# A two-layer diffusion trunk: decay tables and modulation begun in the first stage, HGRN2 scores by halves of a chunk

## The chip, the core and the metric

The kernel runs on one core of a Trainium2 chip. The metric is the device time of one launch in microseconds (us). The core's engines work side by side, each through its own queue in order: PE (TensorE, matrix products), DVE (VectorE), ACT (ScalarE), POOL (GpSimd) and SP (SyncE, which here only issues DMAs). A weight load of PE is shown apart as PEld.

## The reference, cut to what matters

640 tokens (512 latent ones, then a context of 128) pass through two layers of width 1024. In each layer a vector made from a condition (the modulation: six parts of 1024 values, for latents and for context) shifts, scales and gates the stream. Three kinds of heads read one input projection: Fourier mixing, retention, and HGRN2, whose state has a forget gate of its own in every channel. Then come an output projection and a gated feed-forward net.

```python
def _modulation(cvec, w_mod_l, b_mod_l):
    m = jax.nn.silu(cvec) @ w_mod_l + b_mod_l
    return jnp.split(m[..., None, :], N_MOD, axis=-1)

# HGRN2, one chunk: b = running sum of log f
rel = bc[:, :, :, None, :] - bc[:, :, None, :, :]
dec = jnp.exp(jnp.where(tri[:, :, None], rel, -jnp.inf))
A = jnp.sum(qc[:, :, :, None, :] * kc[:, :, None, :, :] * dec, axis=-1)
o = inter + jnp.einsum('bhij,bhjv->bhiv', A, vc)
S = (jnp.exp(b_last[:, :, 0, :])[..., None] * S
     + jnp.einsum('bhjd,bhjv->bhdv', kc * jnp.exp(b_last - bc), vc))
```

Retention has one fixed decay per head and direction instead: `lg = -exp(log_decay)`, from which tables of `exp(distance * lg)` are made. Both run over the sequence forward and backward.

## The kernel before, in words

**Precision.** Most products are made as three matmuls of a high and a low part (`mm3`, L219 to L221). A weight tile is loaded into `wraw` (one of two buffers), ACT casts it to `whi` (L206) and DVE subtracts to get `wlo` (L207). Products in plain f32, those of the HGRN2 and retention heads among them, show two PE records for each call.

**The stages.** The initial stage (`trunk`, from 0 to about 66 us) normalizes the five token tiles, makes shift and scale of layer 0 with matmuls (`weights`, L248), transposes and modulates (`norm`, L371 to L383), and projects the first values (`part`). It goes over four quarters `q` of the width, with five parts in each. Then `mixers` runs the heads of layer 0 (to about 345 us), `feed` the output projection and the feed-forward net; then both again for layer 1, whose mixers lie between about 920 and 1175 us.

**The order.** PE's instructions stay in the order in which the program writes them. The other engines' are put in order by a scheduler, which prefers what the program writes first. The program's order comes from a planner (`Order`, `run_units`): it has a clock `now`, which units of work on PE move on by an estimate (`pe`), and threads, each of which goes on when its due time has come (`due`). The modulation of layer 0's other parts is such a thread: `modulation(0, (2, 3, 4), pace0)` starts at the beginning of `mixers` and takes a step every 2.8 us of the planner's clock. It goes through two halves of the condition; each half has two steps that load and prepare the condition vectors (`csb`, with a sigmoid on ACT into `junk`) and 24 pieces. A piece is a 256 KB load through SP into one of three `wm` buffers and two multiplications with a running sum on DVE (L312, L314).

**HGRN2 scores.** `hgrn` (from L766) is a thread for each of three pairs of heads over the latents (four chunks of 128 tokens, `nu` = 4) and one for the context (three pairs, `nu` = 3). A chunk's 128x128 scores are put together by levels: the diagonal (`pd`, L809), then for `lev` 0 to 6 the scores between neighbouring blocks of 2^lev tokens. At each level PE multiplies the composite keys `C` with the queries `Qx`, 128 columns at a time (L824, one call for each chunk and head: a matmul of 64 rows, 128 weights columns and 128 columns); POOL multiplies the keys and the decay products (L832, L835); ACT makes the next composite (L799); DVE multiplies the queries in place (L839); and of the 128x128 products the blocks that the level is about are put into `AT`: by DVE with a mask for lev 0 to 4 (`copy_predicated`, L843), by ACT block by block for lev 5 and 6 (L847). The next level's matmuls need the `Qx` of L839.

**Decay tables.** `decays` (L656 to L686) is called by the first retention unit in the program's order, in each layer. It loads a small table `ctab` through SP, computes `ea`, `ec`, `gam` and `zt` with exponentials on ACT and small multiplications on DVE (L665 to L675), then the large tables `G` and `DT`.

Of the kernel before, what the change touches and what calls it, by code (L numbers as in the profile page):

```python
# [151 lines left out]
class Kernel:  # L152
    def __init__(self, ctx, tc, a, outs):
        self.tc, self.nc, self.a, self.outs = tc, tc.nc, a, outs
        nc = tc.nc
        PS = bass.MemoryType.PSUM
        self.const = ctx.enter_context(tc.tile_pool(name="const", bufs=1))
        self.wp = ctx.enter_context(tc.tile_pool(name="wp", bufs=1))
        self.actp = ctx.enter_context(tc.tile_pool(name="actp", bufs=1))
        self.psp = ctx.enter_context(tc.tile_pool(name="psp", bufs=8, space=PS))  # L160
        dram = ctx.enter_context(tc.tile_pool(name="dram", bufs=1, space=bass.MemoryType.DRAM))
        self.mem = Slots()
        self.get, self.free, self.can = self.mem.get, self.mem.free, self.mem.can
        self.mem.add(self.wp, "wr", 4096, 2)
        self.mem.add(self.wp, "wh", 4096, 4)
        self.mem.add(self.wp, "wl", 4096, 4)
        self.mem.add(self.actp, "ax", 4 * T, 16)
        self.mem.add(self.actp, "m4", 4096, 8)
        self.xd = dram.tile([T, D], F32, name="xd")
        self.gd = dram.tile([L, 2, 2, D], F32, name="gd")  # L170
        c = self.const

        def load(name, shape, eng=nc.gpsimd):
            t = c.tile(list(shape), F32, name=name)
            eng.dma_start(t, a[name])
            return t

        self.cvec = load("cvec", [128, NK, 2], nc.sync)
        self.ident = load("ident", [128, 128], nc.scalar)
        self.bmf = load("bmf", [128, L, 6, NK], nc.scalar)  # L180
        self.bonesr = c.tile([128, 128], F32R, name="bonesr")
        nc.gpsimd.dma_start(self.bonesr, a["bones"])
        self.bones = self.bonesr.bitcast(F32)
        self.lda = load("lda", [128, L, 2, 6])
        self.ldc = load("ldc", [128, L, 3, 2])
        self.hlb = load("hlb", [128, 2, 2, 3])
        self.mhalf = c.tile([128, 1], F32, name="mhalf")
# [277 lines left out]
    def mixers(self, l, hT, mp):  # L465
# [7 lines left out]
        self.raws, self.mix = [None] * 6, [None] * NK  # L473
        mskf = self.m4("mskf", (128, 7, 128))
        nc.sync.dma_start(mskf, a["masks"])
        self.msk = mp.tile([128, 7, 128], U8, name="msk")
        nc.vector.tensor_copy(self.msk, mskf)
        self.free(mskf)
        self.forget_bounds(l)
        self.PF, self.PK = self.m3("PF", (128, 2, 3, 128)), self.m3("PK", (128, 2, 3, 128))  # L480
# [1 line left out]
        self.Us, self.Up = self.m4("Us", (128, 4, 256)), self.m2("Up", (128, 256))  # L482
        self.hg = {}

        if l == 0:
            o.start(self.modulation(0, (2, 3, 4), P["pace0"], True))
        w = {}

        def half(i, h, name, us):
# [145 lines left out]
    def forget_bounds(self, l):  # L635
# [17 lines left out]
        self.om = mp.tile([128, 2, 3], F32, name="om")  # L653
        nc.vector.tensor_scalar(self.om, self.lb, -1.0, 1.0, ALU.mult, ALU.add)

    def decays(self, l):  # L656
        nc, mp, a = self.nc, self.mp, self.a
        rt = self.m2("rt", (128, 4, 128))
        nc.sync.dma_start(rt, a["rtab"])
        ct_ = mp.tile([128, 2], F32, name="ctab")  # L660
        nc.sync.dma_start(ct_, a["ctab"])
        self.rope = self.m4("rope", (128, 2, 512))
        nc.sync.dma_start(self.rope, a["rope"])
        ea = mp.tile([128, 2, 6], F32, name="ea")
        nc.scalar.activation(out=ea, in_=self.lda[:, l], func=AF.Exp)  # L665
        nc.vector.tensor_scalar(ea, ea, -1.0, None, ALU.mult)
        ec = mp.tile([128, 3, 2], F32, name="ec")
        nc.scalar.activation(out=ec, in_=self.ldc[:, l], func=AF.Exp)
        nc.vector.tensor_scalar(ec, ec, -1.0, None, ALU.mult)
        self.gam = mp.tile([128, 3, 2], F32, name="gam")  # L670
        nc.scalar.activation(out=self.gam, in_=ec, func=AF.Exp, scale=128.0)
        self.zt = mp.tile([128, 2, 6], F32, name="zt")
        for d in range(2):
            nc.vector.tensor_scalar(self.zt[:, d, :], ea[:, d, :], ct_[:, d:d + 1], None, ALU.mult)
        nc.scalar.activation(out=self.zt, in_=self.zt, func=AF.Exp)  # L675
# [90 lines left out]
    def hgrn(self, l, ct):  # L766
# [35 lines left out]

        C = composite(0)
        yield 2.0
        pd = [self.ps("pd") for _ in range(2)]
        for u in range(nu):
            for hh in range(2):
                pr, us = slice(64 * hh, 64 * hh + 64), slice(u * 128, (u + 1) * 128)
                nc.tensor.matmul(pd[hh][:, us], ks[pr, us], q[pr, us], start=True, stop=True)  # L809
        self.o.pe(0.44 * nu)  # L810
        self.free(ks, bases[2])
        for hh in range(2):
            nc.scalar.copy(AT[:, hh], pd[hh][:, 0:W].rearrange("p (u i) -> p u i", u=nu))
        yield 1.0
        S = None
        for lev in range(7):
            s = 1 << lev
            nb = W // s
            np_ = nb // 2
            pl = [self.ps("pl") for _ in range(2)]  # L820
            for u in range(nu):
                for hh in range(2):
                    p0 = 64 * hh
                    nc.tensor.matmul(pl[hh][:, u * 128:(u + 1) * 128], C[p0:p0 + 64, u * 128:(u + 1) * 128],  # L824
                                     pick(Qf, p0, p0 + 64, u * 128, [[2 * s, 64 // s], [W + s, 2], [1, s]]),
                                     start=True, stop=True)
            self.o.pe(0.44 * nu)

            for d in range(2):
# [7 lines left out]
                                  pick(Tt, 0, 128, toff + 1, [[nb, 2], [2, np_]]), ALU.mult)  # L837
            qv = pick(Qf, 0, 128, 0, [[W + s, 2], [2 * s, np_], [1, s]])
            nc.vector.tensor_tensor(qv, qv, pick(Tt, 0, 128, toff + 1, [[nb - 1, 2], [2, np_], [0, s]]), ALU.mult)  # L839
            for hh in range(2):  # L840
                pv = pl[hh][:, 0:W].rearrange("p (u i) -> p u i", u=nu)
                if lev < 5:
                    nc.vector.copy_predicated(AT[:, hh], self.msk[:, lev, :].unsqueeze(1).to_broadcast([128, nu, 128]), pv)  # L843
                else:
                    for b in range(128 // s):
                        rows, cols = (slice(s * i, s * i + s) for i in (b, b ^ 1))
                        nc.scalar.copy(AT[rows, hh, :, cols], pv[rows, :, cols])  # L847
# [434 lines left out]
def trunk(ctx: ExitStack, tc: tile.TileContext, a, outs):  # L1282
# [5 lines left out]
    with tc.tile_pool(name="ini", bufs=1) as ip:  # L1288
        K.VH, K.VR = K.v_tiles(("VH0", "VH1", "VH2")), K.v_tiles(("VR0",))
        cs = K.silu_c(ip)  # L1290
        for kind in ("vh", "vh", "vl", "vl"):
            K.mem.move("m4", kind)
        xts, wms, ws = [], [], []
# [33 lines left out]
        def norm(t, q):  # L1327
            K.norm_T(ip, 0, 0, t, xts[t], hT, t % 2 == 0, ((2 * q, 2),))
# [10 lines left out]
        K.modulation0(K.modulation0_rows(ip, mps[0]), 0)  # L1339
        norm(0, 0)  # L1340
        norm(1, 0)
        for q in range(4):
            for t in range(3):
                norm(t + 2, q)
                part(t, q)
                if q < 3:
                    weights(q + 1, *((0, 1), (2, 3, 4), (5, 6, 7))[t])
            if q < 3:
                rows = K.modulation0_rows(ip, mps[q + 1])
            part(3, q)  # L1350
            if q < 3:
                K.modulation0(rows, q + 1)
                norm(0, q + 1)
                norm(1, q + 1)
            part(4, q)
        K.free(*(t for pair in ws for t in pair), *wmem)
        for kind in ("vh", "vh", "vl", "vl"):
            K.mem.move(kind, "m4")
# [130 lines left out]
```

## Time and profile before

| | |
|---|---|
| median of 3 runs | 1744.54 us (1740.31 to 1745.72) |
| profiled execution, its own time | 1746.83 us |
| its span, first to last instruction | 1745.1 us |
| PE busy | 1683.2 us (96%), 11634 instructions |
| PEld busy | 1547.1 us (89%) |
| DVE busy | 1072.5 us (61%) |
| ACT busy | 694.9 us (40%) |
| POOL busy | 451.5 us (26%) |
| mean granted clock of PE | 0.990 |

The shares are means over all stages. PE's idle time and the stretches in which its clock was granted at less than full are not spread evenly, and a wait that is long on an engine other than PE need not move the end.

### The profile page before, as it was taken

How to read it: one execution, taken by the hardware profiler on the slowest of the kernel's cores; microseconds unless marked ns; L12 is line 12 of the kernel's file. 1: busy time of each engine (PE TensorE's matmuls, PEld its weight loads, DVE VectorE, ACT ScalarE, POOL GpSimd, SP SyncE). 2: the span in 40 equal slices, each digit the busy share in tenths (PEclk: the TensorE clock that was granted, in tenths of full speed). 3: DMA queues.
4: the chain of work that ended last, by engine and by line, in shares of the span. 5: the costliest groups of instructions: out<-in, count | busy, mean ns of one | idle time of the engine just before them, and what ended most of it. 6: DMA issues, size and time to landing. Idle time of an engine off the chain costs nothing.

```text
span 1745.1 us, 29155 instructions
## 1 busy us (share of the span) xinstructions
PE 1683.2 (96%) x11634; PEld 1547.1 (89%) x11634; DVE 1072.5 (61%) x1851; ACT 694.9 (40%) x1362; POOL 451.5 (26%) x473
## 2 busy tenths in 40 slices
PE   6989989999999999999999999999999999999997
PEld 4878878898999999989989998879799999999996
DVE  4597996548668776877484556674654434343428
ACT  4633443745544443434164444367253122121210
POOL 2233432103255453644052233220230000000001
PEclk9999989999999999999999999999999999999999
DMA  8544521242356554544222121113234222222301
GB/s 328 165 129 128 159 63 40 83 169 85 117 190 203 162 181 131 181 135 152 73 101 93 61 74 60 40 59 103 103 109 157 73 73 73 73 85 61 96 26 61
DMA packets 71239, 194.42 MB, mean 111 GB/s; under 512 B 12208, under 2 KB 12992, under 8 KB 71104
## 3 DMA queue, kind: packets, MB, share of 16 engines
q1 hardware_dynamic: 66816, 182.10, 32.5%
q0 software_dynamic: 4000, 10.35, 1.8%
q8 instruction: 91, 1.49, 0.3%
q14 instruction: 44, 0.36, 0.1%
q10 hardware_dynamic: 288, 0.11, 0.0%
HBM read 186.47 MB, written 6.06 MB: 110 GB/s over the span
## 4 chain that ended last, share of the span: by engine, by line
PE 80%; DVE 7%; ACT 3%; issue 2%; POOL 2%; DMA 1%; SPq 0%; DVEq 0%; ACTq 0%; POOLq 0%
PE pg L221 6%; PE pu L221 6%; PE pu L220 6%; PE pu L219 6%; PE pg L220 6%; PE pg L219 6%; PE dps L221 5%; PE dps L220 5%; PE dps L219 5%; PE pl L824 2%; PE p L219 2%; PE ops L221 2%; PE ops L219 2%; PE ops L220 2%; PE p L220 2%
## 5 line engine op out<-in xcount | busy, mean ns | idle before, releaser
L207 DVE TENSOR_TENSOR wlo<-wraw,whi 128x1024 fp32r<-128x1024 f32 x204 | 266.1, 1307 | 255.8 <-ACT whi L206 253.6
L206 ACT CAST whi<-wraw 128x1024 fp32r<-128x1024 f32 x206 | 215.1, 1048 | 405.9 <-PE pg L220 126.2
L316 POOL TENSOR_TENSOR wm<-wm,csb 128x512 f32<-128x512 f32 x112 | 179.8, 1625 | 183.0 <-DVE jb L312 156.8
L221 PE MATMUL pg<-h2T,wlo 128*128 128x384 f32 (+1 forms) x704 | 218.2, 310 | 3.0 <-DVE wlo L207 3.0
L219 PE MATMUL pg<-h2T,whi 128*128 128x384 f32 (+1 forms) x704 | 218.4, 310 | 0.0
L220 PE MATMUL pg<-h2T,whi 128*128 128x384 f32 (+1 forms) x704 | 217.8, 309 | 0.0
L220 PE MATMUL pu<-h2T,whi 128*128 128x384 f32 (+1 forms) x704 | 217.2, 308 | 0.0
L219 PE MATMUL pu<-h2T,whi 128*128 128x384 f32 (+1 forms) x704 | 217.2, 308 | 0.0
L221 PE MATMUL pu<-h2T,wlo 128*128 128x384 f32 (+1 forms) x704 | 217.2, 308 | 0.0
L340 POOL TENSOR_SCALAR bnve<-bnag 128x1 f32<-128x1 f32 x40 | 13.9, 351 | 645.9 <-DVE bnag L338 636.6
L219 PE MATMUL dps<-whi,ah 128*128 128x512 f32 x440 | 171.5, 390 | 0.0
L221 PE MATMUL dps<-whi,al 128*128 128x512 f32 x440 | 171.5, 390 | 0.0
L220 PE MATMUL dps<-wlo,ah 128*128 128x512 f32 x440 | 171.4, 389 | 0.0
L312 DVE SCALAR_TENSOR_TENSOR jb<-wm,csb 128x512 bf16<-128x512 f32 x160 | 149.0, 931 | 14.2 <-DMA wm<-in_w_modT 8.4
L221 PEld LDWEIGHTS pg<-h2T,wlo 128*128 128x128 f32 x704 | 134.0, 190 | 3.5 <-DVE wlo L207 3.4
L219 PEld LDWEIGHTS pg<-h2T,whi 128*128 128x128 f32 x704 | 134.2, 191 | 0.3
L220 PEld LDWEIGHTS pg<-h2T,whi 128*128 128x128 f32 x704 | 134.2, 191 | 0.3
L289 ACT ACTIVATE wm<-wm 128x512 f32<-128x512 f32 x112 | 70.8, 632 | 158.1 <-POOL wm L316 157.8
L221 PEld LDWEIGHTS pu<-h2T,wlo 128*128 128x128 f32 x704 | 133.6, 190 | 0.0
L220 PEld LDWEIGHTS pu<-h2T,whi 128*128 128x128 f32 x704 | 133.6, 190 | 0.0
L219 PEld LDWEIGHTS pu<-h2T,whi 128*128 128x128 f32 x704 | 133.6, 190 | 0.0
L1194 DVE TENSOR_TENSOR sg<-sg,pu 128x256 f32<-128x256 f32 x88 | 42.7, 485 | 119.8 <-PE pu L221 112.9
(273 smaller groups left out, 3830.5 us busy)
## 6 DMA issues: line engine op xcount, KB each, us to landing
wm<-in_w_modT SPq DMA_DIRECT2D x160, 256.0 KB, 2.9
wraw<-in_w_gate SPq DMA_DIRECT2D x44, 512.0 KB, 3.7
wraw<-in_w_up SPq DMA_DIRECT2D x44, 512.0 KB, 3.6
wraw<-in_w_down SPq DMA_DIRECT2D x44, 512.0 KB, 3.6
wraw<-in_w_fm SPq DMA_DIRECT2D x42, 512.0 KB, 3.6
wm<-in_w_mod SPq DMA_DIRECT2D x16, 512.0 KB, 10.2
wraw<-in_w_tm SPq DMA_DIRECT2D x16, 512.0 KB, 3.5
wraw<-in_w_out SPq DMA_DIRECT2D x16, 512.0 KB, 3.7
```

The source lines that it names most:

```text
L206: self.nc.scalar.copy(hi, raw)
L207: (eng or self.nc.vector).tensor_tensor(lo, raw, hi.bitcast(F32), ALU.subtract)
L219: mm(out, lh, rh, start=first, stop=False)
L220: mm(out, lh, rl, start=False, stop=False)
L221: mm(out, ll, rh, start=False, stop=last)
L289: keep(nc.scalar.activation(out=t, in_=t, func=AF.Copy, accum_out=d))
L312: keep(nc.vector.scalar_tensor_tensor(self.jb, wt, 1.0, csb[0], ALU.mult, ALU.mult, accum_out=d[0]))
L316: nc.gpsimd.tensor_tensor(wt, wt, csb[1], ALU.mult)
L340: nc.gpsimd.tensor_scalar(ve, ag[:, 1:2], EPS, None, ALU.add)
L824: nc.tensor.matmul(pl[hh][:, u * 128:(u + 1) * 128], C[p0:p0 + 64, u * 128:(u + 1) * 128], pick(Qf, p0, p0 + 64, u * 128, [[2 * s, 64 // s ...
L1194: nc.vector.tensor_tensor(sg, sg, pu[:, :n], ALU.mult)
```

## The change

**Decay tables.** A new function `decay_rates` is called once, at the head of the initial stage behind `silu_c`, and makes `ea`, `ec`, `gam` and `zt` for both layers in one go. `ctab` becomes a constant that is loaded at the start through POOL's queue. `decays` keeps the loads of `rtab` and `rope` and the large tables.

**Modulation.** The thread `modulation(0, (2, 3, 4), ...)` starts in the initial stage at quarter `q == 2`. After each part, `between` moves the planner's clock on by 2.1 us and lets due threads take steps.

**Scores.** The diagonal and the levels 0 to 5 compute only the two 64x64 diagonal blocks of each 128x128 chunk, and level 6 the two blocks off the diagonal. Each call becomes two: 64 rows, 64 weight columns and 64 columns, the two halves `b` of a chunk going to the lower and the upper 64 partitions of the same bank. `AT` holds them in columns 0 to 63 until level 6, when ACT copies the second half's block to columns 64 to 127, one copy more in each thread. The masked copies are half as wide; the mask is 5x64.

```diff
+        self.ctab = load("ctab", [128, 2])
...
+        self.msk = mp.tile([128, 5, 64], U8, name="msk")
+        for b in (slice(0, 64), slice(64, 128)):
+            nc.vector.tensor_copy(self.msk[b], mskf[b, 0:5, b])
...
-        if l == 0:
-            o.start(self.modulation(0, (2, 3, 4), P["pace0"], True))
...
+    def decay_rates(self):
+        nc, c = self.nc, self.const
+        ea = c.tile([128, L, 2, 6], F32, name="ea")
+        nc.scalar.activation(out=ea, in_=self.lda, func=AF.Exp)
+        nc.vector.tensor_scalar(ea, ea, -1.0, None, ALU.mult)
+        ec = c.tile([128, L, 3, 2], F32, name="ec")
+        nc.scalar.activation(out=ec, in_=self.ldc, func=AF.Exp)
+        nc.vector.tensor_scalar(ec, ec, -1.0, None, ALU.mult)
+        gam = c.tile([128, L, 3, 2], F32, name="gam")
+        nc.scalar.activation(out=gam, in_=ec, func=AF.Exp, scale=128.0)
+        zt = c.tile([128, L, 2, 6], F32, name="zt")
+        for d in range(2):
+            nc.vector.tensor_scalar(zt[:, :, d, :], ea[:, :, d, :], self.ctab[:, d:d + 1], None, ALU.mult)
+        nc.scalar.activation(out=zt, in_=zt, func=AF.Exp)
+        self.rates = (ea, ec, gam, zt)
...
-        ct_ = mp.tile([128, 2], F32, name="ctab")
-        nc.sync.dma_start(ct_, a["ctab"])
...
+        def blocks():
+            for u in range(nu):
+                for hh in range(2):
+                    for b in range(2):
+                        t0 = u * 128 + 64 * b
+                        yield slice(64 * hh, 64 * hh + 64), slice(64 * b, 64 * b + 64), hh, u, b, t0
...
-                    nc.tensor.matmul(pl[hh][:, u * 128:(u + 1) * 128], C[p0:p0 + 64, u * 128:(u + 1) * 128],
-                                     pick(Qf, p0, p0 + 64, u * 128, [[2 * s, 64 // s], [W + s, 2], [1, s]]),
-                                     start=True, stop=True)
+            for pr, rows, hh, u, b, t0 in blocks():
+                if lev < 6:
+                    qs = pick(Qf, pr.start, pr.stop, t0, [[2 * s, 32 // s], [W + s, 2], [1, s]])
+                else:
+                    qs = Qf[pr, (1 - b) * W + t0 + 64 - 128 * b:(1 - b) * W + t0 + 128 - 128 * b]
+                nc.tensor.matmul(pl[hh][rows, u], C[pr, t0:t0 + 64], qs, start=True, stop=True)
...
+            if lev == 6:
+                nc.scalar.copy(A[64:128, :, 64:128], A[64:128, :, 0:64])
...
-                    nc.vector.copy_predicated(AT[:, hh], self.msk[:, lev, :].unsqueeze(1).to_broadcast([128, nu, 128]), pv)
+                    nc.vector.copy_predicated(AT[:, hh, :, 0:64], self.msk[:, lev, :].unsqueeze(1).to_broadcast([128, nu, 64]),
+                                              pl[hh])
...
+        K.decay_rates()
...
+        def between():
+            K.o.pe(2.1)
+            K.o.due()
+
         for q in range(4):
+            if q == 2:
+                K.o.start(K.modulation(0, (2, 3, 4), P["pace0"], True))
             for t in range(3):
                 norm(t + 2, q)
                 part(t, q)
+                between()
...
             part(3, q)
+            between()
...
             part(4, q)
+            between()
```

## Rows read from the trace of the kernel before

**Rows 1.** Busy time by stage: stretch, its length, engines busy (instructions), PEclk, DMA, GB/s.

```profile
66.00:100.00 34.00, 34.00 (x261) 33.38 (x260) 15.78 (x35) 16.59 (x39) 10.83 (x16) 1.00 0.48 150
100.00:260.00 160.00, 139.31 (x1163) 126.42 (x1163) 144.13 (x302) 63.60 (x148) 62.19 (x74) 0.95 0.39 122
960.00:1175.00 215.00, 210.38 (x1968) 187.36 (x1967) 130.87 (x240) 99.63 (x231) 69.15 (x92) 0.99 0.20 60
```

**Rows 2.** The same view in stretches of 20 us (PE, PEld, DVE, ACT, POOL, PEclk).

```profile
40.00:60.00 20.00, 18.71 (x163) 13.49 (x162) 12.58 (x30) 11.39 (x23) 2.72 (x4) 1.00 0.61 183
...
120.00:140.00 20.00, 17.37 (x135) 16.20 (x132) 18.00 (x40) 9.32 (x29) 3.88 (x4) 0.91 0.53 159
...
160.00:180.00 20.00, 15.96 (x137) 15.10 (x137) 16.38 (x35) 5.09 (x9) 4.68 (x6) 0.91 0.35 112
...
220.00:240.00 20.00, 15.47 (x118) 14.23 (x116) 19.90 (x53) 6.42 (x15) 6.90 (x9) 0.83 0.21 64
240.00:260.00 20.00, 16.73 (x134) 15.24 (x134) 17.66 (x25) 9.45 (x25) 8.16 (x9) 0.92 0.17 54
```

**Rows 3.** PE's waits, 66 to 345 us: who waited for whom, us, times, longest.

```profile
PE pl L824 <- DVE Qx L839: 17.9, 12, 3.5
```

**Rows 4.** PE's waits, 900 to 1175 us (layer 1): the one wait of a score matmul.

```profile
PE pl L824 <- ACT K L512: 0.7, 1, 0.7
```

**Rows 5.** DVE in order of time around 101 us: start, length, line, operation.

```profile
101.09 1.04 DVE L314 SCALAR_TENSOR_TENSOR jb<-wm,csb 128x512 bf16<-128x512 f32 x1
...
102.67 0.67 DVE L839 TENSOR_TENSOR Qx<-Qx,F 128x512 f32<-128x512 f32 x1
```

**Rows 6.** DVE in order of time, 68 to 89 us; in brackets the idle time before.

```profile
76.24 0.36 DVE L674 TENSOR_SCALAR zt<-ea,ctab 128x6 f32<-128x6 f32 x2 [8.26 <-DMA ctab<-in_ctab]
80.67 2.36 DVE L207 TENSOR_TENSOR wlo<-wraw,whi 128x1024 fp32r<-128x1024 f32 x2 [4.06 <-ACT whi L206]
88.41 0.42 DVE L522 TENSOR_TENSOR q<-q,p 128x256 f32<-128x256 f32 x1 [5.39 <-ACT q L521]
```

**Rows 7.** PE in order of time, four stretches: groups of small matmuls (xcount is records).

```profile
29.19 0.86 PE L248 MATMUL modps<-wm,cs 128*32 128x128 f32 x24
...
103.39 1.23 PE L824 MATMUL pl<-Qx,C 64*128 64x128 f32 x16 [1.68 <-DVE Qx L839]
...
144.59 0.92 PE L697 MATMUL U<-VH,KT 128*64 128x64 f32 x24
...
1081.85 1.16 PE L824 MATMUL pl<-Qx,C 64*128 64x128 f32 x16
...
1086.01 1.16 PE L824 MATMUL pl<-Qx,C 64*128 64x128 f32 x16
```

**Rows 8.** Line 248 alone in 0.05 us stretches (matmuls in flight, then weight loads).

```profile
29.20:29.25 0.05, 0.05 (x4) 0.05 (x8) 1.00 0.41 164
...
29.30:29.35 0.05, 0.05 (x8) 0.05 (x11) 1.00 0.83 328
```

**Rows 9.** Groups by line and shape, 0 to 400 us: count, busy us, mean ns, idle.

```profile
L312 DVE SCALAR_TENSOR_TENSOR jb<-wm,csb 128x512 bf16<-128x512 f32 x48 | 37.5, 781 | 0.7 <-DMA wm<-in_w_modT 0.3
...
L824 PE MATMUL pl<-Qx,C 64*128 64x128 f32 x420 | 34.2, 303 | 18.0 <-DVE Qx L839 17.9
...
L843 DVE COPY_PREDICATED AT<-msk,pl 128x512 f32<-128x512 uint8 x30 | 21.0, 723 | 0.0
...
L799 ACT COPY C<-K 128x512 f32<-128x512 f32 x21 | 14.0, 668 | 20.2 <-POOL K L832 9.6 <-PE pl L824 8.6 <-PE fp L220 2.1
...
L843 DVE COPY_PREDICATED AT<-msk,pl 128x384 f32<-128x384 uint8 x10 | 5.6, 582 | 2.5 <-PE pl L824 2.5
```

**Rows 10.** DMA issues of the first 20 us: size and us to landing.

```profile
lda<-in_lda POOLq DMA_DIRECT2D x1, 12.0 KB, 7.0
```

**Rows 11.** ACT in order of time, the first normalizations.

```profile
12.09 7.16 ACT L1318 ACTIVATE x<-x,bnnm,bnrs 128x512 f32<-128x512 f32 x10 [8.92 <-DVE bnnm L348]
```

**Rows 12.** PE in order of time, the longest stall of the quarters q = 2 and 3.

```profile
57.45 0.50 PE L219 MATMUL tps<-whi,hT 128*128 128x512 f32 x1 [1.10 <-ACT hT L382]
```

More of the change, by code (lines that the diff above doesn't have):

```diff
@@ L475, in mixers @@
         nc.sync.dma_start(mskf, a["masks"])
-        self.msk = mp.tile([128, 7, 128], U8, name="msk")
-        nc.vector.tensor_copy(self.msk, mskf)
+        self.msk = mp.tile([128, 5, 64], U8, name="msk")
+        for b in (slice(0, 64), slice(64, 128)):
+            nc.vector.tensor_copy(self.msk[b], mskf[b, 0:5, b])
         self.free(mskf)
@@ L659, in decays @@
         nc.sync.dma_start(rt, a["rtab"])
-        ct_ = mp.tile([128, 2], F32, name="ctab")
-        nc.sync.dma_start(ct_, a["ctab"])
         self.rope = self.m4("rope", (128, 2, 512))
         nc.sync.dma_start(self.rope, a["rope"])
[L664 to L675, printed above, removed]
+        ea, ec, self.gam, self.zt = (t[:, l] for t in self.rates)
         self.G = self.m3("G", (128, 3, 2, 128))
@@ L804, in hgrn, with halves @@
         yield 2.0
[L805 to L809, printed above, removed]
+        A = AT.rearrange("p h u i -> p (h u) i")
+        def halves(name):
+            return [self.ps(name)[:, 0:W // 2].rearrange("p (u i) -> p u i", u=nu) for _ in range(2)]
+        def blocks():
[4 more added lines that the diff above has]
+                        yield slice(64 * hh, 64 * hh + 64), slice(64 * b, 64 * b + 64), hh, u, b, t0
+        pd = halves("pd")
+        for pr, rows, hh, u, b, t0 in blocks():
+            nc.tensor.matmul(pd[hh][rows, u], ks[pr, t0:t0 + 64], q[pr, t0:t0 + 64], start=True, stop=True)
         self.o.pe(0.44 * nu)
@@ L812, in hgrn @@
         for hh in range(2):
-            nc.scalar.copy(AT[:, hh], pd[hh][:, 0:W].rearrange("p (u i) -> p u i", u=nu))
+            nc.scalar.copy(AT[:, hh, :, 0:64], pd[hh])
         yield 1.0
@@ L819, in hgrn @@
             np_ = nb // 2
[L820 to L823, printed above, removed]
-                    nc.tensor.matmul(pl[hh][:, u * 128:(u + 1) * 128], C[p0:p0 + 64, u * 128:(u + 1) * 128],
-                                     pick(Qf, p0, p0 + 64, u * 128, [[2 * s, 64 // s], [W + s, 2], [1, s]]),
-                                     start=True, stop=True)
+            pl = halves("pl")
+            for pr, rows, hh, u, b, t0 in blocks():
+                if lev < 6:
[3 more added lines that the diff above has]
+                nc.tensor.matmul(pl[hh][rows, u], C[pr, t0:t0 + 64], qs, start=True, stop=True)
             self.o.pe(0.44 * nu)
@@ L839, in hgrn @@
             nc.vector.tensor_tensor(qv, qv, pick(Tt, 0, 128, toff + 1, [[nb - 1, 2], [2, np_], [0, s]]), ALU.mult)
+            if lev == 6:
+                nc.scalar.copy(A[64:128, :, 64:128], A[64:128, :, 0:64])
             for hh in range(2):
-                pv = pl[hh][:, 0:W].rearrange("p (u i) -> p u i", u=nu)
                 if lev < 5:
-                    nc.vector.copy_predicated(AT[:, hh], self.msk[:, lev, :].unsqueeze(1).to_broadcast([128, nu, 128]), pv)
-                else:
-                    for b in range(128 // s):
-                        rows, cols = (slice(s * i, s * i + s) for i in (b, b ^ 1))
-                        nc.scalar.copy(AT[rows, hh, :, cols], pv[rows, :, cols])
+                    nc.vector.copy_predicated(AT[:, hh, :, 0:64], self.msk[:, lev, :].unsqueeze(1).to_broadcast([128, nu, 64]),
+                                              pl[hh])
+                elif lev == 5:
+                    for b in range(4):
+                        rows, cols = slice(32 * b, 32 * b + 32), slice(32 - 32 * (b % 2), 64 - 32 * (b % 2))
+                        nc.scalar.copy(AT[rows, hh, :, cols], pl[hh][rows, :, cols])
+                else:
+                    for b in range(2):
+                        rows = slice(64 * b, 64 * b + 64)
+                        nc.scalar.copy(AT[rows, hh, :, 64 - 64 * b:128 - 64 * b], pl[hh][rows])
             Tt, toff, tnext = Tn, tnext, tnext + 2 * np_
```

## The prediction

> **What bounds the kernel now.** I read the busy shares first: PE is busy for 96% of the span, so only what shortens PE's own work or its stalls can move the end. Next come the windows by stage. From 66 to 100 us PE has no gap. From 100 to 260 us, under the HGRN2 levels of layer 0, it is busy for 139.31 of 160 us, and DVE for 144.13 [rows 1]. That is 20.7 us of idle PE, the largest loss in one place. The same heads in layer 1 (960 to 1175 us) leave 4.6 us in 215, with DVE at 61% [rows 1].
>
> In the 20 us windows the idle time has a second price: the granted clock reads 0.91, 0.91, 0.83 and 0.92 in the four windows in which PE stalled most [rows 2]. A reading below 1 is a mean of the two levels, 1.2 and 2.4 GHz. Against 1.00 it makes (0.09 + 0.09 + 0.17 + 0.08) x 20 = 8.6 us. So up to 20.7 + 8.6 = 29.3 us are to be had in this stage.
>
> The waits say what PE stood for: 17.9 us in 12 waits for the query multiplication L839 on DVE [rows 3]. In layer 1 no score matmul waits for it; the one wait there is 0.7 us for ACT [rows 4]. What layer 1 lacks is the modulation on DVE. In order of time one sees it directly: an L314 of the modulation ends just before the masked copies and the Qx of 102.67 us [rows 5], and PE's level at 103.39 us had stood for 1.68 us [rows 7].
>
> Before that, DVE stands idle: 8.26 us until ctab lands, 4.06 us for a cast that was queued on ACT behind the same table, 5.39 us for the projection of q [rows 6]. These 17.7 us would take a quarter of the modulation (48 pieces, below); it cannot use them, since the queue is in order and zt stands at its head.
>
> **Part 1: decay tables first.** The chain ctab, zt goes from 68 to 77 us, and with it 8.26 us of idle DVE and most of the 4.06 us. PE has no gap there [rows 1], so this pays nothing by itself: it gives DVE room for modulation, counted in part 2. At the start the new work is four small exponentials with a table load on ACT and four small multiplications on DVE. ACT idles 8.92 us until 12.09 us [rows 11]; lda takes 7.0 us to land and so is there at about 9 us [rows 10], ctab, behind it in the same queue, somewhat later. That hides it, unless the scheduler puts DVE's part ahead of the first statistics; these are then late by the tables' landing at most, 7 us. I take 0.5 lost; a gain is excluded, since nothing is taken away there.
>
> **Part 2: modulation begun in quarter 2.** Ten parts of 2.1 us of the planner's clock, 21 us, lie before the mixers now: 21 / 2.8 = 7.5 steps. A piece is two multiplications of 0.78 us [rows 9] (L314 is L312's twin), 1.56 us.
>
> In the quarters this puts perhaps three more pieces on DVE than run there now, 4.7 us, and some steps of ACT and SP. DVE is busy for 12.58 of 20 us there and PE for 18.71 [rows 2]; PE's longest stall, 1.10 us, is for the chain of transposes, casts and differences [rows 12], and a multiplication in its way delays it by up to 0.8 us. Bounds: nothing, and all 4.7 us plus some clock. I take 2 us lost. The moved 256 KB loads pass SP after all loads of the initial stage; those of the first projections come after them, but PE reaches these only at 66 us.
>
> In the mixers the gain is worked out for one level. In layer 1 levels lie 4.16 us apart (1081.85 to 1086.01 us) [rows 7]. In that time the modulation's pace asks 4.16 / 2.8 = 1.5 pieces of DVE, 2.34 us; two masked copies 1.45 us [rows 9]; Qx 0.67 us [rows 5]; and the differences of weights 0.78 us (1.18 us each [rows 6], one for a projection of 48 matmuls, of which 261 take 34 us [rows 1], so one in 6.3 us). Together 5.24 us, 1.08 more than there is. After the change the copies have half the elements. From 512 elements in 723 ns and 384 in 582 ns [rows 9] the slope is 1.10 ns, so 256 take 441 ns, two 0.88 us. The sum is 4.67 us, 0.51 over. Besides, the thread lasts 54 steps of 2.8 us, 151 us, of which 21 lie before the mixers: 14% fewer levels lie beside it. What is over falls to 0.51 x 0.86 / 1.08 = 0.41 of what it was. Of the 17.9 us of waits and 8.6 us of clock, 59% are 15.6 us. I take 13: DVE remains the later one in these levels, and the change of halves, with its sigmoid on ACT, stays in the queue. Bounds: 4 and 26.5 us. Late next is DVE still, and after the modulation PE itself.
>
> **Part 3: scores in 64 columns.** On DVE 30 copies save 0.28 us and 10 save 0.21 us in each layer; this is in part 2 for layer 0 and nothing in layer 1, where no PE wait ends on DVE [rows 4]. ACT gains one copy of 64 partitions x 512 in each of four threads, near 0.67 us [rows 9]; at 63.60 of 160 us [rows 1] it hides that. It waits for the same masked copies as the block copies beside it did, so it adds no wait of its own.
>
> On PE 16 records become 32 of half the columns. Now a group of 16 takes 1.16 us [rows 7], of which one record's own length is 0.30 [rows 9]: (1.16 - 0.30) / 16 = 54 ns a record, two tiles of the array (upper and lower rows) side by side. With 64 columns and two tiles, L697 takes (0.92 - 0.30) / 24 = 26 ns; with 128 columns and four tiles, L248 takes (0.86 - 0.30) / 24 = 23 ns (its records may be a little shorter) [rows 7]. Halving the columns halves it, and doubling the tiles halves it. The new form has both: 13.5 ns if nothing else limits, 27 ns if records cannot follow each other faster. No group here is faster than 23 ns; but in L248 the matmuls in flight go from 4 to 8 within 0.1 us, and 8 weight loads are in flight early on [rows 8], so four starts come close together. I take 20 ns: 32 x (27 - 20) = 0.22 us saved per group of four chunks, 0.17 for the context; bounds 0 and 0.43. A thread has the diagonal and seven levels, so a layer saves 8 x (3 x 0.22 + 0.17) = 6.6 us.
>
> In layer 1 PE is never without work, and the 6.6 us count. In layer 0 most groups stand in the stage that DVE sets, where a shorter group only waits longer; I count a third, 2 us.
>
> The Trainium skill has a rule that speaks against this part: "TensorEngine Tiling (Array Packing)", section Instruction Overhead, says that each matmul costs about 60 cycles however few columns it has, and advises against tiling a dimension that is small already. By it a record cannot come under 25 ns (an estimate from the page's 60 cycles at 2.4 GHz), a group saves 32 x (27 - 25) = 0.06 us, and the part is worth some 2.5 us in all. No row here tests 64 columns on four tiles. The same page's Key Properties say that tiles load weights and multiply independently, and by that the full halving would come. Rivals 1 and 2 below are these two, from rows alone.
>
> **Sum.** The profiled execution took 1746.8 us: 1746.8 + 0.5 + 2 - 13 - 2 - 6.6 = 1727.7 us. It lies 2.3 us above the median of the runs shown, so I predict 1727.
>
> **Rivals.**
> Rival 1, records cannot follow faster than 27 ns (L248 and L697 end near one value though their tiles and columns differ, which speaks for a common floor; the simultaneous starts speak against). The scores then give PE nothing, and only the queue's relief remains: 1727 + 8.6 = 1736 us, between 1728 and 1744.
> Rival 2, four tiles run fully side by side, 13.5 ns: layer 1 gains 8 x (3 x 0.43 + 0.32) = 12.9 us, layer 0 some 4: 1727 - 8.3 = 1719 us.
> Rival 3, the modulation doesn't get ahead, or costs what it returns: its loads share DMA engines that are busy to 0.61 in these quarters [rows 2], its multiplications stand before the chain of the quarters. Loss 8 us in place of 2 there (4.7 us and a lower clock), gain 7 in place of 13: 1727 + 12 = 1739 us. For it: DVE must fit 4.7 us into quarters with short waits already [rows 12]; against it: 18 us of empty DVE follow at once [rows 6].
> Rival 4, slower: the change of tile on every record costs PE time, since the four blocks of a chunk alternate between all four tiles. At 40 ns a record a group loses 32 x 13 = 0.42 us, both layers 8 x 2 x (3 x 0.42 + 0.31) = 25 us where 8.6 were gained: 1727 + 8.6 + 25 = 1761 us. The other parts give 10.5 us over 8 x 2 x (3 x 32 + 24) = 1920 records, so it decides from 27 + 5.5 = 32 ns on. Against it: L248 alternates between four tiles without such a price [rows 7].
>
> **Chances.** Forecast 0.47 (its own range 1717 to 1737), rival 1 0.20, rival 2 0.13, rival 3 0.11, rival 4 0.09. What a measurement can tell from no change is 0.3%, 5.2 us: faster means below 1739.3, slower above 1749.8. Faster: nearly all of the forecast, 0.7 of rival 1, all of rival 2, half of rival 3: 0.78. Slower: rival 4 and a little of rival 3: 0.10. Same: 0.12. The range 1713 to 1744 leaves out rival 4 and the far ends.
>
> **What would show it.** In the trace after: no wait of zt for ctab near 70 us, and modulation multiplications between 66 and 88 us, eight or so; the wait of L824 for Qx down from 17.9 to some 7 us, the clock windows at 0.95 or more; the stage from 100 to 260 us shorter by some 13 us; masked copies of 0.44 us; a group of 32 score records in layer 1 at 0.85 to 1.0 us (at 1.16: rival 1; 0.73: rival 2; 1.6: rival 4). The prediction is wrong if the quarters 2 and 3 stretch by more than 5 us, if the waits for Qx stay, or if the groups on PE grow.

## The result

The changed kernel takes 1717.99 us, the median of 4 runs (1717.00 to 1719.44), against 1742.58 us for the kernel before (4 runs, 1740.31 to 1745.72). The ratio is 0.9847, 95% interval 0.9829 to 0.9864: 24.6 us, or 1.5%, faster. That is 9 us under the forecast of 1727, inside its range and almost at the figure of rival 2 (1719). The interval lies wholly under 1, so the kernel is faster.

A profiled execution lies some us from its kernel's median: the one of before took 1746.8 us, 4.2 above, the one of after 1719.4 us, 1.5 above. The stretch from the heads of layer 0 to layer 1 holds the same PE work in all fourteen profiled kernels and took 561.8 to 565.0 us. So a stage of one profile tells differences of about 3 us or more, and all differences to the kernel before may be up to 4 us too large. Stages are cut at PE's first matmul of a kind: the first projection of a layer (`p`), the first output projection (`ops`), and the first projection of the second layer. "Heads" is from `p` to `ops`: the HGRN2 levels with everything beside them.

| profiled, us | initial | heads, layer 0 | from there to layer 1 | heads, layer 1 | rest |
|---|---|---|---|---|---|
| before | 65.98 | 304.76 | 563.59 | 280.43 | 530.34 |
| after | 68.57 | 289.71 | 562.45 | 266.59 | 530.38 |
| difference | +2.59 | -15.05 | -1.14 | -13.84 | 0 |

The two head stages as windows (columns as in [rows 1]: PE, PEld, DVE, ACT, POOL busy, the granted clock, DMA), before:

```profile
65.98:370.74 304.76, 282.70 (x2417) 258.41 (x2415) 227.38 (x455) 143.74 (x306) 89.68 (x111) 0.97 0.34 105
934.33:1214.76 280.43, 275.81 (x2418) 252.79 (x2417) 161.43 (x278) 142.59 (x296) 77.44 (x104) 0.99 0.21 64
```

and after:

```profile
68.57:358.28 289.71, 266.52 (x2897) 243.27 (x2895) 215.39 (x453) 144.54 (x306) 91.56 (x111) 0.98 0.34 109
920.73:1187.32 266.59, 259.57 (x2898) 238.11 (x2896) 151.81 (x278) 143.17 (x300) 77.62 (x104) 1.00 0.21 67
```

The length minus PE's busy time is PE's idle time. In layer 0 it is 304.76 - 282.70 = 22.06 us before and 23.19 after; in layer 1 4.62 and 7.02. In neither stage did PE's idle time fall: its busy time fell by 16.2 us in each. The groups of score matmuls alone, levels and diagonal, were busy for 38.65 us before and 22.89 after in layer 0 (15.8 less), and for 37.25 and 22.19 in layer 1 (15.1 less).

Of the 13.84 us of layer 1, 1.6 are the clock. The stage comes in two lengths with the same work: in kernels with the old scores 280.43 and 280.37 us at a granted clock of 0.99 (before, and tables alone) and 278.82 and 278.87 at 1.00 (tables and modulation together, and modulation alone); with the change's scores 268.14 and 268.16 at 0.99 and 266.59 and 266.58 at 1.00. At either clock the new scores take 12.2 to 12.3 us off. One of each, tables and modulation with the old scores at 1.00, and scores and modulation at 0.99:

```profile
927.93:1206.75 278.82, 274.20 (x2418) 251.17 (x2417) 161.31 (x278) 142.42 (x296) 77.23 (x104) 1.00 0.20 64
922.47:1190.61 268.14, 261.12 (x2897) 239.59 (x2896) 151.84 (x278) 143.24 (x300) 77.72 (x104) 0.99 0.20 67
```

The rows that answer to [rows 1] and [rows 2]:

```profile
66.00:100.00 34.00, 34.00 (x268) 33.32 (x268) 25.11 (x65) 11.76 (x32) 10.54 (x15) 1.00 0.58 189
100.00:260.00 160.00, 144.26 (x1752) 130.31 (x1751) 135.90 (x304) 69.83 (x164) 67.55 (x76) 0.98 0.36 116
960.00:1175.00 215.00, 207.98 (x2421) 187.39 (x2421) 128.67 (x245) 121.24 (x258) 66.20 (x88) 1.00 0.20 65
...
120.00:140.00 20.00, 17.22 (x182) 16.20 (x182) 16.01 (x33) 9.32 (x25) 4.73 (x5) 0.91 0.46 152
220.00:240.00 20.00, 16.42 (x217) 15.26 (x218) 16.83 (x27) 9.93 (x25) 7.99 (x9) 0.91 0.16 54
280.00:300.00 20.00, 15.38 (x186) 13.75 (x174) 10.95 (x23) 9.18 (x26) 5.05 (x6) 0.83 0.16 53
```

DVE's work moved as the change says: 9.3 us more from 66 to 100 us, 8.2 less from 100 to 260. PE's waits from 66 to 345 us (who waited for whom, us, times, longest) answer to [rows 3]:

```profile
PE pl L842 <- DVE Qx L855: 10.9, 7, 2.8
PE pr L928 <- DVE rx L542: 7.1, 3, 4.6
PE o L741 <- DVE S L717: 1.8, 2, 1.0
```

The waits for Qx fell by 7.0 us, but `pr` (scores of the retention heads), which waited 3.7 us before, waits 7.1, and `o` (output of the heads), which did not wait, 1.8. Before:

```profile
PE pr L906 <- DVE rx L542: 3.7, 2, 2.7
```

In layer 1 [rows 4] the score matmuls now wait for DVE, 2.4 us, which is what PE's idle time grew by there:

```profile
PE pr L928 <- DVE rx L542: 2.9, 2, 1.9
PE pl L842 <- DVE Qx L855: 2.4, 4, 1.2
```

DVE in order of time, in place of the idle stretches of [rows 6]: modulation pieces start at 66.30, 68.85, 70.47, 73.98, 76.60, 78.06, 80.55 and 82.01 us, and no zt stands there any more.

```profile
66.30 0.69 DVE L313 SCALAR_TENSOR_TENSOR jb<-wm,csb 128x512 bf16<-128x512 f32 x1
...
73.98 0.69 DVE L313 SCALAR_TENSOR_TENSOR jb<-wm,csb 128x512 bf16<-128x512 f32 x1 [1.50 <-DMA wm<-in_w_modT]
...
82.01 0.69 DVE L313 SCALAR_TENSOR_TENSOR jb<-wm,csb 128x512 bf16<-128x512 f32 x1
```

PE's groups of score matmuls (xcount is records, the PE instructions of the trace, two for each call), answering to the 1.16 us of [rows 7]:

```profile
130.63 0.69 PE L842 MATMUL pl<-Qx,C 64*64 64x64 f32 x32
...
288.07 0.58 PE L842 MATMUL pl<-Qx,C 64*64 64x64 f32 x24
...
1072.68 0.69 PE L842 MATMUL pl<-Qx,C 64*64 64x64 f32 x32 [0.35 <-DVE Qx L855]
```

The groups by shape, here of the whole run (count, busy us, mean ns, idle), answering to [rows 9]:

```profile
L842 PE MATMUL pl<-Qx,C 64*64 64x64 f32 x1680 | 39.8, 231 | 13.4 <-DVE Qx L855 13.2
...
L860 DVE COPY_PREDICATED AT<-msk,pl 128x256 f32<-128x256 uint8 x60 | 25.2, 441 | 7.4 <-PE pl L842 7.4
...
L860 DVE COPY_PREDICATED AT<-msk,pl 128x192 f32<-128x192 uint8 x20 | 6.9, 368 | 9.3 <-PE pl L842 9.3
```

ACT at the start ([rows 11]), with the small exponentials ahead of the first normalization:

```profile
7.68 0.22 ACT L660 ACTIVATE ea<-lda 128x24 f32<-128x24 f32 x1 [3.22 <-DMA lda<-in_lda]
...
12.64 7.16 ACT L1341 ACTIVATE x<-x,bnnm,bnrs 128x512 f32<-128x512 f32 x10 [2.93 <-DVE bnnm L349]
```

### The profile page after: what moved, and what is told of

Same layout as the page of the kernel before. It is cut to its first block, busy times and chain, and to the rows that moved or that the text cites. A ratio compares the mean times of both kernels' runs of the same rounds, so it can differ in the third digit from the quotient of the medians.

```text
span 1717.7 us, 31084 instructions
## 1 busy us (share of the span) xinstructions
PE 1651.0 (96%) x12594; PEld 1517.4 (88%) x12594; DVE 1056.3 (61%) x1849; ACT 698.5 (41%) x1368; POOL 452.5 (26%) x474
```

## The experiments

Each kernel was timed beside the kernel before; ratios are to that, with the 95% interval. First the parts one by one, put into the kernel before.

**Scores alone**: the 64-column scores, the half-width masks, masked copies and block copies; tables and modulation stay as they were.

```diff
+        pd = halves("pd")
+        for pr, rows, hh, u, b, t0 in blocks():
+            nc.tensor.matmul(pd[hh][rows, u], ks[pr, t0:t0 + 64], q[pr, t0:t0 + 64], start=True, stop=True)
...
+                    nc.vector.copy_predicated(AT[:, hh, :, 0:64], self.msk[:, lev, :].unsqueeze(1).to_broadcast([128, nu, 64]), pl[hh])
```

> The scores part alone on the kernel before (tables and modulation as they were). Theory 1, four tiles: a group of 32 records takes 0.69 us in place of 1.16, the heads of layer 1 (first projection to first output projection, 280.4 us before) shorten by 13 to 14 us, and those of layer 0 (304.8 us) by some 4, since DVE's queue still sets them: 1742.6 - 18 = 1725 us. Rival 1, masked copies: it is DVE's shorter copies that count; then layer 0 shortens by 10 or more and layer 1, where no matmul waits for DVE, hardly: 1732 us. Rival 2, the parts need each other (PE faster finds only a longer queue in layer 0): layer 0 keeps its 305 us: 1729 us.

Measured 1719.44 us, 0.9862 [0.9842, 0.9881]. Its two head stages:

```profile
65.77:356.51 290.74, 269.84 (x2897) 247.59 (x2895) 218.69 (x456) 144.57 (x310) 93.75 (x111) 0.96 0.34 110
918.40:1187.85 269.45, 262.48 (x2898) 240.96 (x2897) 152.18 (x281) 143.47 (x302) 77.58 (x104) 0.99 0.21 68
```

and its waits from 66 to 345 us:

```profile
PE pl L837 <- DVE Qx L850: 14.8, 10, 3.4
PE pr L923 <- DVE rx L543: 5.1, 2, 3.0
```

This part by itself gives the whole gain, as far as the intervals tell. None of the three expectations came out: theory 1 had layer 1 about right and gave layer 0 only 4 us, rival 1 had layer 0 right and gave layer 1 hardly any, rival 2 left layer 0 as it was, and both stages got shorter, by 14.0 and 11.0 us. PE does the same work in layer 1 in this kernel and the changed one: 262.48 and 259.57 us busy with the same instructions, which differ by 2.9 us with the clock at 0.99 and 1.00.

**Tables first and modulation in the quarters, without the scores.**

```diff
+        K.decay_rates()
...
+            if q == 2:
+                K.o.start(K.modulation(0, (2, 3, 4), P["pace0"], True))
```

> Decay tables first and modulation begun at quarter 2, scores as before. Theory of the forecast: layer 0 heads shorten by 13 us, the initial stage grows by 2.6, layer 1 stays: 1742.6 - 10.5 = 1732 us, waits for Qx down to some 7 us. Rival, the scores made layer 0 shorter: this kernel gains 0 to 3 us in layer 0 and loses 2.6 at the start: 1742 us, waits for Qx still above 13 us.

Measured 1742.30 us, 0.9993 [0.9982, 1.0004], 12 runs: no difference, as the rival had it. Its head stage of layer 0 and its waits from 66 to 345 us:

```profile
68.78:365.92 297.14, 279.88 (x2416) 254.72 (x2415) 222.35 (x452) 144.42 (x302) 92.15 (x111) 0.98 0.34 105
```

```profile
PE pl L827 <- DVE Qx L842: 8.2, 8, 1.9
PE pr L909 <- DVE rx L541: 6.0, 3, 4.4
PE o L740 <- DVE S L716: 1.1, 2, 0.9
```

The waits for Qx fall from 17.9 to 8.2 us, to about the 7 us of the forecast and not, as the rival had it, to 13 or more; PE's idle time in the stage falls only from 22.06 to 17.26, since `pr` and `o` wait longer. The stage is 7.6 us shorter than in the profile of before, of which the initial stage takes 2.8 back; but this profile lies 3.5 us under its kernel's median, and that of before 4 over, so 1 us in the medians is what stands.

**Tables alone, and modulation alone**: one of the two hunks above each.

```diff
 # tables alone
+        K.decay_rates()
 # modulation alone
+                K.o.start(K.modulation(0, (2, 3, 4), P["pace0"], True))
```

> Decay tables first, nothing else. If the 8.3 us that zt stood at the head of DVE's queue were room that modulation can use: layer 0 shortens by 3 to 6 us, 1738 us. If that room is worth nothing until the modulation is begun earlier: 1742 us, within 2 us of before. In either case a start later by 0 to 1 us.

> Modulation begun at quarter 2, nothing else. If getting ahead counts by itself: layer 0 shortens by 6 to 10 us, the initial stage grows by 2: 1736 us. If zt at the head of DVE's queue near 70 us still holds the pieces up: no more than 3 us from layer 0, 1742 us.

Tables alone 1747.63 us, 1.0023 [1.0008, 1.0037]; modulation alone 1741.18 us, 0.9983 [0.9969, 0.9996] (12 runs each). Both lie within the 0.3% that count as no change; the tables lean to the slow side and the modulation to the fast side. Their initial stages took 70.13 and 66.51 us, where before took 65.98: the tables' start is later by 4 us and not by 0 to 1. The heads of layer 0 took 303.97 and 301.16 us. So the tables gave the modulation no room that counts by itself, and of the modulation alone the second expectation came out.

**The order of the calls**: in the changed kernel the two halves of a chunk become the outermost loop, so that successive matmuls take turns on two tiles of the array (upper and lower rows) and no longer on four. The work is the same.

```diff
-            for u in range(nu):
-                for hh in range(2):
-                    for b in range(2):
+            for b in range(2):
+                for u in range(nu):
+                    for hh in range(2):
```

> The changed kernel with the lower halves of all chunks first and then the upper ones, so that only two tiles of the array (upper and lower rows) take turns; same 32 records, same short copies. Theory 1, four tiles side by side: a group goes back to about 32 x 27 + 300 = 1.16 us, the heads of layer 1 (266.6 us) grow by some 13 us and those of layer 0 (289.7 us) by as much as PE's share of their gain: if PE's shorter groups made all of it, 14, if DVE's shorter copies made it, under 4. Totals 1745 or 1735 us. Rival, half columns alone make the group short whatever the order: 0.69 us stays, 1718 us.

Measured 1727.42 us, 0.9910 [0.9894, 0.9927], 9 us slower than the change. The two head stages, and one group on PE:

```profile
68.48:358.18 289.70, 272.44 (x2897) 249.66 (x2896) 212.69 (x453) 144.88 (x306) 91.95 (x111) 0.98 0.32 108
920.11:1194.85 274.74, 269.12 (x2898) 247.80 (x2896) 152.26 (x278) 143.37 (x300) 76.45 (x104) 0.99 0.19 64
```

```profile
1073.28 0.97 PE L842 MATMUL pl<-Qx,C 64*64 64x64 f32 x32
```

The levels' score groups of layer 1 alone (length, PE busy, clock), after and here:

```profile
920.73:1187.32 266.59, 19.53 (x840) 1.00 0.21 67
920.11:1194.85 274.74, 26.85 (x840) 0.99 0.19 64
```

The group grows from 0.69 to 0.97 us, more than half of the way back to 1.16, so the rival is out and theory 1 is right in part: half of the columns on two tiles already saves 0.19 us. In layer 1 the score groups are busy 7.3 us longer in the levels and 1.0 in the diagonal (3.67 for 2.66). The stage grows by 8.15 us against the changed kernel, but 1.6 of it are the clock: against the 268.14 us that the same heads take at 0.99 it is 6.6, since PE's idle time fell by 1.4. In layer 0, at 0.98 in both, PE is busy 5.92 us longer and idle 5.93 us less: 289.70 us against 289.71. There a longer group only fills a wait.

**The masked copies done twice**, in the changed kernel.

```diff
+                    for _ in range(2):
-                    nc.vector.copy_predicated(AT[:, hh, :, 0:64], ...)
+                        nc.vector.copy_predicated(AT[:, hh, :, 0:64], ...)
```

> The changed kernel with each masked copy on DVE done twice, which gives back the copies' old time on DVE (two of 0.44 us for one of 0.72) and leaves PE's groups short. If shorter copies made the gain in layer 0: its heads grow from 289.7 us by 8 us or more, 1727 us. If PE's shorter groups made it: by under 3 us, 1719 us. Layer 1 stays in either case, since no score matmul waits for DVE there.

Measured 1725.48 us, 0.9895 [0.9875, 0.9916], 7.5 us slower than the change. The heads took 292.15 us in layer 0 (+2.4) and 269.57 in layer 1 (+3.0), the initial stage 69.78 (+1.2); no stage is beyond the edge of what one profile tells. At the same clock (0.99) layer 1 is 1.4 us longer, with 8.26 us of idle PE in place of 7.02, so there too the copies cost a little, which the expectation excluded. The total came near the first expectation (1727) and layer 0 near the second (under 3 us); this run does not decide between them.

**Scores and modulation, tables as before; and everything, with the call that makes the tables written at the end of the initial stage.**

```diff
 # scores and modulation, as against the full change
-        self.ctab = load("ctab", [128, 2])
-        K.decay_rates()
 # tables at the end, as against the full change
-        K.decay_rates()
...
+        K.decay_rates()
         K.free(*(t for pair in ws for t in pair), *wmem)
```

> Scores and modulation, the decay tables as before. The tables cost the initial stage 2 to 4 us and gave layer 0 little: 1716 us, 2 us under the changed kernel. If the tables are what lets the modulation run between 66 and 88 us: layer 0 loses 3 us or more, 1720 us.

> The changed kernel with the tables computed at the end of the initial stage in place of its head (ctab still loaded at the start). If the head of ACT's and DVE's queues is what made the initial stage longer: it shrinks from 68.6 to some 66.5 us and the rest stays, 1716 us. If the modulation in the quarters made it longer: 68 us stay, 1718 us.

Measured 1717.82 us, 0.9859 [0.9837, 0.9882], and 1720.84 us, 0.9872 [0.9852, 0.9892]. The tables moved to the start give nothing on top of the other two parts. The initial stages: 66.76 us without them, 68.11 with the call written last, 68.57 with it first.

The second of these is no test of later tables. The scheduler put their work at the head all the same: `ea` starts at 7.47 us, in the changed kernel at 7.68.

```profile
7.47 0.22 ACT L660 ACTIVATE ea<-lda 128x24 f32<-128x24 f32 x1 [3.00 <-DMA lda<-in_lda]
```

So no run shows what tables computed later would cost, and neither expectation of this run was tested.

**The same two edits on the scores alone**, to see them without the queue's relief.

```diff
 # e9: scores alone
+                    for _ in range(2):
 # e10: scores alone
+            for b in range(2):
+                for u in range(nu):
+                    for hh in range(2):
```

> Scores alone (modulation and tables as before), each masked copy on DVE done twice. In layer 0 the scores alone took 14 us from the heads (304.8 to 290.7 us). If DVE's shorter copies made that: 8 us or more come back, 299 us or more, 1730 us. If PE's shorter groups made it: under 4 us come back, 1723 us. Layer 1 grows by 3 us as it did in the changed kernel with copies done twice.

> Scores alone, lower halves first, then upper (a group of 32 records 0.97 us in place of 0.69). If the group on PE stands in a loop with DVE's multiplication (group, Qx, next group), each of 28 groups gives its 0.28 us back in layer 0: 290.7 + 8 = 299 us. If DVE's queue sets the stage: layer 0 stays within 2 us of 290.7. Layer 1 grows by 8 us either way: 1736 or 1728 us.

Measured 1726.19 us, 0.9899 [0.9884, 0.9913], and 1727.04 us, 0.9909 [0.9896, 0.9922]. The head stage of layer 0 with the copies doubled:

```profile
65.52:362.84 297.32, 269.85 (x2896) 245.92 (x2895) 231.56 (x496) 143.97 (x310) 93.72 (x111) 0.96 0.33 108
```

and with two tiles alternating:

```profile
64.69:356.57 291.88, 274.98 (x2896) 252.90 (x2895) 219.05 (x456) 144.74 (x310) 95.65 (x111) 0.97 0.33 110
```

Against the scores alone (290.74 us, 269.84 busy) the doubled copies add 6.6 us, all of it idle PE, which lies between the two expectations (8 or more, under 4); the slower groups add 5.1 us of busy PE and 1.1 us of length, as the second expectation had it. In layer 1 it is the reverse: against the 268.14 us of the scores at the same clock, 269.58 us with doubled copies and 274.86 with the slower groups.

**A slower modulation**: its pace goes from 2.8 to 3.6 us, first with scores and modulation start, then with the scores alone. The idea was that DVE has fewer pieces to do between two levels.

```diff
-pace0=2.8
+pace0=3.6
```

> Scores and modulation begun at quarter 2, one step every 3.6 us of the planner in place of 2.8. If DVE is asked for too much while modulation and levels run together: waits for Qx fall from 11 us by half and layer 0 shortens by 4 to 6 us, 1713 us. If stretching it only puts the same multiplications under more levels: 1718 us.

> Scores alone with the modulation's step every 3.6 us. If DVE is asked for too much: layer 0 shortens by 4 to 6 us against scores alone, 1714 us. If not, or if the modulation then reaches into the retention heads behind: 1719 us or more.

Measured 1734.64 us, 0.9950 [0.9936, 0.9963], and 1730.82 us, 0.9929 [0.9917, 0.9941]: 17 and 11 us slower than with 2.8, where the expectations had a gain or no change. The second of them, from 200 to 260 us:

```profile
200.00:260.00 60.00, 38.81 (x614) 34.16 (x614) 57.77 (x148) 25.20 (x63) 28.90 (x36) 0.77 0.26 88
```

Its second pair of heads began 78.6 us after the first projection, against 81.9 with the scores at 2.8, so the early levels did gain. But now the modulation reaches the last heads, where DVE is full (57.77 of 60 us), PE stands for 21 us, and the clock falls to 0.77. None of the twelve kernels is measurably faster than the change; the simplest that equal it are the scores alone and the scores with the modulation.

## Why the prediction was right, and what in it was not

**The bound and the stages.** By stage the sum had +2.5 for the initial stage, -15 for the heads of layer 0 and -6.6 for those of layer 1, together -19.1. Measured: +2.6, -15.05, and -13.84, of which 12.3 are the change and the rest the clock. Against the 24.6 us between the medians the sum is 5.5 short, and layer 1 accounts for it (12.3 for 6.6). The other 3.5 of the 9 us lie in where the forecast started: it counted from a profile that lay 4.2 us over the median of its kernel and took off only 0.7, although it put that profile 2.3 over the median itself.

That layer 0 came out at -15 is in part luck. Its 13 were to come out of PE's waits and its clock. Scores alone took 14 us off the heads of layer 0 with the waits for Qx still at 14.8 us and the clock at 0.96; the queue's two other parts by themselves brought those waits to 8.2 us and hardly moved the time (0.9993). The copies, from which nearly all of the 13 was to come, account for half of the 14 us or less (below).

**The term that was mis-sized: a group's saving.** I took 20 ns a record, between 13.5 and 27, and so 0.22 us a group. By the forecast's own formula, with the 0.23 us that a record has by itself (231 ns mean), it is (0.69 - 0.23) / 32 = 14 ns, and a group saves 1.16 - 0.69 = 0.47 us. The group of a context went from 0.94 us to 0.58 us, 0.36 saved. That makes 8 x (3 x 0.47 + 0.36) = 14.2 us a layer in place of 6.6; the trace has 15.1 us less of busy score groups in layer 1. The stage got 12.3 us shorter, since 2.4 us came back as waits of these groups for Qx on DVE: that PE is never without work there, on which the forecast counted the saving in full, no longer held. Rival 2 had this size, and rivals 1 (27 ns) and 4 (40 ns) are refuted. What I leaned on was that no group of the profile was faster than 23 ns a record; these had either two tiles or 128 columns, and the evidence for the full halving, eight matmuls in flight at once [rows 8], was in the same rows. The order of the calls shows why: with two tiles alternating a record takes (0.97 - 0.23) / 32 = 23 ns, with four 14 ns. In layer 1, where PE has little idle time, this 0.28 us a group came back as 6.6 us of the stage at the same clock.

The rule of the Trainium skill that was weighed ("TensorEngine Tiling (Array Packing)", section Instruction Overhead), some 60 cycles for each matmul, would make a group of 32 at least 32 x 25 = 800 ns long (an estimate from that page), and the part worth 2.5 us. This trace does not agree: 0.69 us for the whole group. Key Properties of the same page of the Trainium skill, by which tiles load and multiply independently, do agree here, as long as the calls go round all four tiles.

**"In the stage that DVE sets a shorter group only waits longer"** held as far as it was tested. The groups of layer 0 saved as much PE time as those of layer 1, twice what was forecast, and the stage was no shorter than forecast: PE's idle time there stayed at 23 us, although the queue was relieved. The order experiment shows it directly (289.70 against 289.71 us). The limit of this: with the copies doubled in the scores alone, which puts DVE's work per level above that of before (two copies of 0.44 us for one of 0.72), the stage was still 7.4 us shorter than the profile of before, of which some 3 us can be that profile's distance from its median. So it looks as if the levels are not set by DVE's work alone, and the steps from Qx over the group to the copy count too; that was not shown. How they share the 14 us was not settled: the copies' time is worth 6.6 us with the scores alone and 2.4 in the changed kernel, a group longer by 0.28 us 1.1 and nothing, and no run has the new scores with both the long copies and the long groups.

**The queue's relief, -13.** In its working nearly all came from the half-width copies. The copies took 441 and 368 ns, as the slope of [rows 9] said, but of the 14 us that the scores alone bring in layer 0 the doubled copies give back 6.6, half of what the term needs. The modulation's lead and the tables by themselves are worth 1 us in the medians, and on top of the scores nothing that the intervals show. Two readings under this term were wrong. The levels of layer 1 do not lie 4.16 us apart throughout, but 5.48 and 4.16 in turn, so by the same working DVE lacks about 0.9 us a level on average and not 1.08:

```profile
1091.49 1.16 PE L824 MATMUL pl<-Qx,C 64*128 64x128 f32 x16
```

And the four windows of lower clock are not the four in which PE stalled most: from 100 to 120 us it stood for 3.9 us at 1.00, longer than from 120 to 140 us (2.6 us at 0.91).

```profile
100.00:120.00 20.00, 16.12 (x141) 14.90 (x141) 19.88 (x36) 6.14 (x11) 7.30 (x8) 1.00 0.41 116
```

The thread's 54 steps are 52 (two halves of 2 + 24), which changes nothing. What failed, too, is the sign by which I would know it: the Qx waits were to fall to 7 us and the clock windows to rise to 0.95. With the queue parts alone the waits did fall to 8.2, and the time hardly moved; with the full change they are 10.9, and windows at 0.91 and 0.83 remain. Part of the waits that went came back at the next consumers: with the queue parts alone `pr` and `o` wait 3.4 us longer. Of the modulation by itself rival 3 was near the truth in that it returns little, but not by its price: it was to lose 8 us in the quarters, and they are hardly longer.

**The initial stage.** +2.6 us as summed, but split the other way round. Where neither tables nor modulation are moved, five profiles have 64.69 to 65.98 us; with the modulation's start moved and the tables not, three have 65.62 to 66.76, so it adds 1 us or less, where I had put 2. With the tables, six have 68.11 to 70.13: they add 2 to 4, where I had put 0.5. That term looked at the start alone, and there the first normalization did slip, from 12.09 to 12.64 us, with 0.7 us of DVE's small multiplications standing ahead of statistics. The larger part shows at its end. PE waits 1.19 and 0.67 us for the chain of `hT` (the input made ready for the projection), where before it waited 1.10 once, and then its clock falls. Its second wait, and the window behind it, after and before:

```profile
60.00 0.50 PE L222 MATMUL tps<-whi,hT 128*128 128x512 f32 x1 [0.67 <-DVE hT L384]
60.00:64.00 4.00, 4.00 (x12) 3.12 (x13) 2.64 (x6) 2.95 (x7) 0.35 (x1) 0.57 0.59 195
...
60.00:64.00 4.00, 3.99 (x19) 2.93 (x18) 3.99 (x15) 3.72 (x11) 1.24 (x1) 1.00 0.35 109
```

At 0.57 these 4 us lose (1 - 0.57) x 4 = 1.7 us. All six kernels with the tables at the start have 0.57 to 0.78 in this window, and all eight without them 1.00. Why work at 8 to 10 us brings a wait at 59 us is open; no run separates it.

## What to carry to other kernels

Cutting small matmuls into halves paid in full here when the calls went round all four tiles of the array (0.47 us a group) and less than half of it on two in turn (0.19 us), so the loop order is part of the change. What it pays at the end is decided by the stage: some 15 us of shorter groups made the stage 12.3 us shorter where PE sets the pace, and where DVE sets it a longer group cost 0 to 1 us. A wait that vanishes is no gain until the idle time of the whole stage has fallen; add up PE's busy and idle time between two fixed marks before counting single waits. Compare a stage with one of the same granted clock: between 0.99 and 1.00 lay 1.6 us of layer 1. And where a scheduler orders the work, look in the trace whether a moved call moved anything.

## What was not expected of the hardware

By the group's length less one record, records of 64 columns followed each other every 14 ns on four alternating tiles and every 23 ns on two, the same instructions in another order; before, records of 128 columns on two tiles took 54 ns. With the slower modulation the granted clock fell to a mean of 0.77 over 60 us in which PE was busy for 38.81; with the modulation begun early as well it was 0.75 from 180 to 240 us, and no kernel at the old pace went below 0.83 over such a stretch.
